# Another order of loads in the opening of a streaming encoder step: input rows first, scale vectors by ScalarE's queue, weight pieces split on ScalarE

## The chip, the cores and the metric

The kernel runs on one core of one Trainium2 chip. Its time is the device time of one execution in microseconds (us); the time before is the median of three runs. The profile is one further execution, with the hardware profiler on. TensorE (PE) multiplies matrices, VectorE (DVE), ScalarE (ACT) and GpSimd (POOL) work element by element, and SyncE (SP) issues most of the transfers (DMA). Matrices come from on-chip SBUF and their products go to PSUM banks.

## The reference

A two-layer streaming encoder, for a prompt of 1024 rows and for 8 running streams of 16 rows each (together one more tile of 128 rows, the "sample" tile). All is float32.

```python
def project_a(x, g_norm, w_qkv, g_q, g_k):            # layer 0
    qkv = rmsnorm(x, g_norm) @ w_qkv                  # 1024 -> 1024 q + 256 k + 256 v
    q, k, v = jnp.split(qkv, ...)
    return rmsnorm(q per head, g_q), rmsnorm(k per head, g_k), v

for layer in range(2):
    # layer 0: window attention with distance penalty and learned sinks, own chunk of 64 rows + 2 before
    # layer 1: own q; K/V computed once from the layer's input; own chunk + 8 before; relative bias
    hp = hp + attention(hp) @ w_o                     # prompt, hs the same with the cached keys
    hp = hp + jnp.square(jax.nn.relu(rmsnorm(hp, g_mlp) @ w_up)) @ w_down
```

`rmsnorm(x, g)` is `x * rsqrt(mean(x*x) + 1e-6) * g`. The outputs are the two streams' rows and the new keys and values.

## The kernel before

The 1024 prompt rows are eight tiles of 128 rows (0 to 7), the sample tile is number 8 (`ST`). To keep float32 accuracy each operand of a product is split in an upper part of reduced mantissa (`hh`, or `w[:, 0]`) and the rest (`hl`, `w[:, 1]`), and a product is three matmuls: upper by upper, upper by rest, rest by upper.

A layer has an attention stage (`attention`), an output projection (`wo_phase`) and an MLP (`mlp_up`, `mlp_down`). The change concerns the opening of layer 0's attention, between the program's start and about 55 us.

The opening goes so. `prep_gains` loads the five scale vectors in five transfers (L1153), has TensorE turn them (`ps_g`) and VectorE copy them to `gcol`, one column for each block of 128 features. `X(t)` loads the rows of tile t (L1331). `N(t)` has TensorE turn them, eight transposes into two PSUM banks `ps_n` (L191), has ScalarE and VectorE split them into `hh` and `hl` (L109, L115), and takes the sum of squares on ScalarE (L182, `junk`). `load_block` loads 1024x512 weights as four transfers of 512 KB into four buffers `raw` and `raw2` and splits each with `split_g`: the scaled upper part on GpSimd (L166), the rest on VectorE (L171). `K1(t)` is the K/V projection of a tile, 8 chunks of three matmuls (L198, L199, L200) into a bank `ps_mm`, followed by the work that empties this bank: V to `VS` on ScalarE and VectorE (L257, L258), K to `kw` twice on ScalarE (L264, L265), and its norm. `Q1(t, 0)` is the projection of the first half of the heads, with weights `wq[0]`, followed by its own norm. K1 of tiles 0, 1 and ST run chunk by chunk together, and then Q1 of the three one after the other. K1(0) and Q1(0) use the one bank of the role `m`, the others the two banks of the role `s`. `K2` and `Q2` turn K and Q. `spill(t)` writes `hh` and `hl` to DRAM (`hTd`, L1361) for the second half of the heads later on. `sinks` loads the constants `cst` and the sinks, and prepares `usink`, `susink` and others for the scores. `unit` is the attention of a pair of sample streams; it loads cached keys and values (`kc`, `vc`).

The order in which each engine gets its instructions is not the text's order: a scheduler sets it by a timeline of its own, from data dependencies, priorities and `behind(a, b)`, which puts instruction b after a in that timeline without a wait on the chip. Each engine then runs its own list strictly in order. SP, too, issues its transfers in order, and an issue waits until its buffer is free and until the transfer eight before it has landed.

Of the kernel before, what the change touches and what calls it, by code (L numbers as in the profile page):

```python
# [75 lines left out]
class Build:  # L76
# [45 lines left out]
    def load_block(self, dst, w, n0, g, ks=range(0, KC, 2), act=False):  # L122
        nc = self.nc
        wr = w.rearrange("(k p) n -> p k n", p=P)
        for k0 in ks:
            raw = self.raw([P, 2, 512])
            nc.sync.dma_start(raw, wr[:, k0 : k0 + 2, n0 : n0 + 512])
            split = lambda k0=k0, raw=raw: self.split_g(
                dst[:, 0, k0 : k0 + 2, :], dst[:, 1, k0 : k0 + 2, :], raw, g, k0, act
# [31 lines left out]
    def split_g(self, hi, lo, raw, g, k0, act):  # L161
        nc = self.nc
        for k in range(raw.shape[1]):
            s = self.gcol[:, g * KC + k0 + k : g * KC + k0 + k + 1]
            if "g" in self.engs and not act:
                nc.gpsimd.tensor_scalar(hi[:, k], raw[:, k], s, 1.0, ALU.mult, ALU.mult)  # L166
            else:
                z = nc.scalar.activation(hi[:, k], raw[:, k], AF.Copy, scale=s)
                if act:
                    self.behind(self.lp, z)  # L170
# [347 lines left out]
    def unit(self, up, small, layer, bp, j, v8, gq8, cache_k, cache_v):  # L518
        nc = self.nc
        kc = up.tile([P, 2, HD], F32, tag="kc", name="kc")  # L520
        nc.sync.dma_start(kc, cache_k[2 * bp : 2 * bp + 2, :, j, :].rearrange("b k d -> k b d"))
        vc = up.tile([P, 2, HD], F32, tag="vc", name="vc")
        nc.sync.dma_start(vc, cache_v[2 * bp : 2 * bp + 2, :, j, :].rearrange("b k d -> k b d"))
# [620 lines left out]
    def prep_gains(self):  # L1144
        nc, I = self.nc, self.ins
        with ExitStack() as st:
            self.psum_pools(st, "pg", dict(m=(1, 1)), dict(m="m"))
            tmp = self.pool(st, "tmpg")
            g = tmp.tile([5 * KC, P], F32, tag="g", name="g")
            for i, v in enumerate(  # L1150
                (I["g_attn"][0], I["g_attn"][1], I["g_mlp"][0], I["g_mlp"][1], I["g_kv"])
            ):
                nc.sync.dma_start(g[i * KC : (i + 1) * KC, :], v.rearrange("(k p) -> k p", p=P))  # L1153
            ps = self.psum("m", [P, 5 * KC], "ps_g")
            nc.tensor.transpose(ps, g, self.ident[0 : 5 * KC, 0 : 5 * KC])
            nc.vector.tensor_copy(self.gcol, ps)
# [11 lines left out]
    def run(self):  # L1168
# [9 lines left out]
        with ExitStack() as top:  # L1178
# [40 lines left out]
            self.prep_gains()  # L1219
# [31 lines left out]
    def sinks(self, ring):  # L1251
        nc, I = self.nc, self.ins
        self.cst = ring.tile([P, C_W], F32, tag="cst", name="cst")
        nc.sync.dma_start(self.cst, I["consts"])
        self.sink = ring.tile([P, H], F32, tag="sink", name="sink")
        nc.sync.dma_start(self.sink, I["sink_a"][0].partition_broadcast(P))
        self.usink = ring.tile([P, H], F32, tag="usink", name="usink")
        nc.vector.tensor_tensor(self.usink, self.sink, self.cst[:, C_ISL : C_ISL + H], ALU.mult)
# [3 lines left out]
        for i in range(G):  # L1262
            nc.sync.dma_start(
                self.ssink[i * 32 : i * 32 + 32, :],
                sk[i : i + 13 : 4].partition_broadcast(32),
            )
        self.nslope = ring.tile([P, KV], F32, tag="nslope", name="nslope")
# [6 lines left out]
    def attention(self, layer):  # L1274
# [18 lines left out]
        with ExitStack() as st:  # L1293
# [307 lines left out]
            if 1 in psp:  # L1601
                wq[0] = self.wslot()
                for k0 in range(0, KC, 2):
                    self.load_split(wq[0], 1, [k0, k0 + 1])
# [202 lines left out]
```

## Time and profile before

| | |
|---|---|
| median of 3 runs | 2391.8 us (2388.46 to 2393.51) |
| the profiled execution | 2387.86 us |
| its span, first to last instruction | 2386.1 us |
| TensorE busy | 2313.9 us, 97% of the span |
| VectorE, ScalarE, GpSimd busy | 1627.6, 1216.5, 540.8 us |
| mean rate of all transfers | 161 GB/s |

A row of a timeline gives start, length, engine, source line, operation and tiles, and in brackets how long the engine stood idle before it and what released it. A row "0.00:50.00" of a table by stretches gives the length of the stretch, the busy time of PE, PE's weight loads, DVE, ACT and POOL with the number of instructions, the granted TensorE clock as a share of full speed, the busy share of the DMA engines and their GB/s. "SPq" and "ACTq" rows are the issue of a transfer, not the transfer. A matmul's row is longer than its distance to the next, since matmuls overlap.

### The profile page before, as it was taken

How to read it: one execution, taken by the hardware profiler on the slowest of the kernel's cores; microseconds unless marked ns; L12 is line 12 of the kernel's file. 1: busy time of each engine (PE TensorE's matmuls, PEld its weight loads, DVE VectorE, ACT ScalarE, POOL GpSimd, SP SyncE). 2: the span in 40 equal slices, each digit the busy share in tenths (PEclk: the TensorE clock that was granted, in tenths of full speed). 3: DMA queues.
4: the chain of work that ended last, by engine and by line, in shares of the span. 5: the costliest groups of instructions: out<-in, count | busy, mean ns of one | idle time of the engine just before them, and what ended most of it. 6: DMA issues, size and time to landing. Idle time of an engine off the chain costs nothing.

```text
span 2386.1 us, 33438 instructions
## 1 busy us (share of the span) xinstructions
PE 2313.9 (97%) x11621; PEld 1931.7 (81%) x11621; DVE 1627.6 (68%) x3002; ACT 1216.5 (51%) x2423; POOL 540.8 (23%) x828
## 2 busy tenths in 40 slices
PE   7998999899999999999999999998999999999999
PEld 6787877788888878888778788887888888888887
DVE  6788786655565776776577876877555565777674
ACT  3777674555555432332267666665555555323321
POOL 4334332311221100000333444444111211000000
PEclk9999999999999999999999999999999999999999
DMA  7335545343443964333653655554443445734332
GB/s 258 119 108 169 170 146 200 129 146 126 157 146 123 356 213 149 119 128 109 232 153 112 198 166 167 168 168 169 142 142 129 158 145 203 274 133 159 117 113 115
DMA packets 217529, 383.78 MB, mean 161 GB/s; under 512 B 50248, under 2 KB 124944, under 8 KB 210192
## 3 DMA queue, kind: packets, MB, share of 16 engines
q1 hardware_dynamic: 194288, 305.08, 38.9%
q0 software_dynamic: 21776, 71.84, 7.8%
q10 hardware_dynamic: 1296, 4.72, 0.5%
q8 instruction: 92, 1.51, 0.3%
q14 instruction: 77, 0.63, 0.1%
HBM read 245.42 MB, written 135.09 MB: 159 GB/s over the span
## 4 chain that ended last, share of the span: by engine, by line
PE 79%; DVE 7%; DMA 7%; ACT 3%; issue 2%; POOL 1%; SPq 1%; ACTq 0%; DVEq 0%; POOLq 0%
PE ps_x L727 9%; PE ps_x L729 9%; PE ps_x L728 9%; PE ps_y L729 7%; PE ps_y L728 7%; PE ps_y L727 7%; PE ps_mm L198 3%; PE ps_mm L200 3%; PE ps_mm L199 3%; PE ps_tr L305 2%; PE ps_mm L157 1%; PE ps_mm L158 1%; PE ps_mm L159 1%; PE ps_s L729 1%; PE ps_s L728 1%
## 5 line engine op out<-in xcount | busy, mean ns | idle before, releaser
L109 ACT CAST w<-r 128x2048 fp32r<-128x2048 f32 x56 | 107.1, 1913 | 325.2 <-PE ps_y L729 213.0
L727 PE MATMUL ps_x<-w,s 128*128 128x512 f32 x512 | 199.6, 390 | 4.2 <-DVE hc L866 2.1
L729 PE MATMUL ps_x<-w,s 128*128 128x512 f32 x512 | 199.4, 389 | 0.0
L728 PE MATMUL ps_x<-w,s 128*128 128x512 f32 x512 | 199.3, 389 | 0.0
L198 PE MATMUL ps_mm<-w,hh 128*128 128x512 f32 x432 | 172.5, 401 | 7.3 <-POOL w L166 3.2
L200 PE MATMUL ps_mm<-w,hl 128*128 128x512 f32 x432 | 172.1, 399 | 1.6 <-DVE hl L115 0.8
L199 PE MATMUL ps_mm<-w,hh 128*128 128x512 f32 x432 | 170.9, 397 | 1.3 <-DVE w L171 1.1
L109 ACT CAST s<-s 128x2048 fp32r<-128x2048 f32 x56 | 107.1, 1913 | 118.1 <-DMA s<-hd 109.3
L115 DVE TENSOR_TENSOR w<-r,w 128x2048 fp32r<-128x2048 f32 x56 | 128.2, 2290 | 51.0 <-ACT w L109 51.0
L727 PE MATMUL ps_x<-sx,w 128*128 128x512 f32 (+1 forms) x408 | 157.9, 387 | 3.9 <-ACT hc L846 3.0
L1033 DVE TENSOR_TENSOR x<-ps_y,x 128x512 f32<-128x512 f32 x136 | 92.4, 687 | 100.8 <-PE ps_y L729 100.8
L729 PE MATMUL ps_x<-sx,w 128*128 128x512 f32 (+1 forms) x408 | 154.2, 378 | 0.0
L728 PE MATMUL ps_x<-sx,w 128*128 128x512 f32 (+1 forms) x408 | 154.1, 378 | 0.0
L109 ACT CAST w<-ru 128x512 fp32r<-128x512 f32 (+1 forms) x160 | 110.0, 708 | 85.5 <-PE ps_y L728 32.0
L729 PE MATMUL ps_y<-w,s 128*128 128x512 f32 x384 | 149.5, 389 | 0.0
L727 PE MATMUL ps_y<-w,s 128*128 128x512 f32 x384 | 149.4, 389 | 0.0
L728 PE MATMUL ps_y<-w,s 128*128 128x512 f32 x384 | 149.4, 389 | 0.0
L115 DVE TENSOR_TENSOR s<-s 128x2048 fp32r<-128x2048 f32 x56 | 128.0, 2286 | 29.1 <-ACT s L109 28.9
L115 DVE TENSOR_TENSOR ptl<-ps_tr,pth 128x512 fp32r<-128x512 f32 x180 | 122.5, 685 | 24.1 <-ACT pth L109 17.8
L115 DVE TENSOR_TENSOR w<-ru,w 128x512 fp32r<-128x512 f32 (+1 forms) x160 | 126.5, 793 | 11.2 <-ACT w L109 11.1
L115 DVE TENSOR_TENSOR wq<-ru,wq 128x1024 fp32r<-128x1024 f32 x32 | 39.7, 1240 | 131.9 <-ACT wq L109 131.9
L109 ACT CAST pth<-ps_tr 128x512 fp32r<-128x512 f32 x180 | 104.9, 595 | 45.0 <-PE ps_tr L305 36.7
(280 smaller groups left out, 6579.7 us busy)
## 6 DMA issues: line engine op xcount, KB each, us to landing
s<-hd SPq DMA_DIRECT2D x56, 1024.0 KB, 4.7
ru<-in_w_up SPq DMA_DIRECT2D x64, 512.0 KB, 4.0
r<-in_w_down SPq DMA_DIRECT2D x32, 1024.0 KB, 5.8
hd<-hc POOLq DMA_DIRECT2D x128, 256.0 KB, 2.7
hd<-hs POOLq DMA_DIRECT2D x96, 256.0 KB, 2.5
x<-xd SPq DMA_DIRECT2D x41, 512.0 KB, 4.4
o<-oTd SPq DMA_DIRECT2D x52, 256.0 KB, 5.0
xd<-xo SPq DMA_DIRECT2D x18, 512.0 KB, 2.8
```

The costliest lines, as they stand in the source:

```text
L109: a = nc.scalar.copy(hi, src)
L115: return a, e.tensor_tensor(lo, src, hi.bitcast(F32), ALU.subtract)
L157: nc.tensor.matmul(ps, oh[:, k, :], w[:, 0, k, nn], start=(k == 0), stop=False)
L158: nc.tensor.matmul(ps, oh[:, k, :], w[:, 1, k, nn], start=False, stop=False)
L198: nc.tensor.matmul(ps, a, w[:, 0, k, :], start=(k == 0), stop=False)
L199: nc.tensor.matmul(ps, a, w[:, 1, k, :], start=False, stop=False)
L200: self.lp = nc.tensor.matmul(ps, b, w[:, 0, k, :], start=False, stop=(k == KC - 1))
L305: self.lp = nc.tensor.transpose(pt[:, i, :], get(i), self.ident)
L727: a = mm(ps, ah, bh, start=first, stop=False, skip_group_check=True)
L728: mm(ps, ah, bl, start=False, stop=False, skip_group_check=True)
L729: return a, mm(ps, al, bh, start=False, stop=last, skip_group_check=True)
L1033: tt(xs[t][:, N[n]], ps, xs[t][:, N[n]], ALU.add)
```

## The change

It moves the scale vectors out of a stage of their own: three transfers (two vectors each, and one) are issued by ScalarE's queue, after which SP's first transfers are the identity and tile 0. They are turned only after tile 0's rows. The weights for K/V come as pieces of 256 KB (`parts=2`), in turn with the rows of tiles 0, 1 and ST, and ST has a buffer of its own. In layer 0 the upper parts of all weights are now scaled on ScalarE instead of GpSimd (`eng='cu'`). Constants, rows of tiles 2 and 3, sinks, spills of tiles 0, 1, ST and the caches are put behind the last weight transfer (`self.gate`), in layer 1 the caches and the MLP's scale vector as well. Sinks are prepared after Q1(1).

```diff
     def load_block(self, dst, w, n0, g, ks=range(0, KC, 2), parts=1):
...
-            nc.sync.dma_start(raw, wr[:, k0 : k0 + 2, n0 : n0 + 512])
+            for k in range(0, 2, 2 // parts):
+                z = slice(k, k + 2 // parts)
+                self.gate = nc.sync.dma_start(raw[:, z], wr[:, k0 : k0 + 2, n0 : n0 + 512][:, z])
...
-            if "g" in self.engs and not act:
+            if "g" in self.engs:
                 nc.gpsimd.tensor_scalar(hi[:, k], raw[:, k], s, 1.0, ALU.mult, ALU.mult)
             else:
                 z = nc.scalar.activation(hi[:, k], raw[:, k], AF.Copy, scale=s)
-                if act:
+                if self.pace:
                     self.behind(self.lp, z)
...
+    def load_gains(self, pool):
+        g = pool.tile([5 * KC, P], F32, tag="pvt", name="g", bufs=1)
+        n = 2 * KC
+        for i, v in enumerate((I["g_attn"], I["g_mlp"])):
+            nc.scalar.dma_start(g[i * n : (i + 1) * n, :], v.rearrange("l (k p) -> (l k) p", p=P))
+        nc.scalar.dma_start(g[2 * n :, :], I["g_kv"].rearrange("(k p) -> k p", p=P))
...
             if A:
+                g = self.load_gains(apool)
                 X(0)
-                self.load_block(wkv, wkv_src, kv0, gkv, [0])
+                N(0)
+                self.turn_gains(g)
+                self.load_block(wkv, wkv_src, kv0, gkv, [0], 2)
                 X(1)
-                N(0)
-                self.load_block(wkv, wkv_src, kv0, gkv, [2])
+                self.load_block(wkv, wkv_src, kv0, gkv, [2], 2)
                 X(ST)
                 N(1, "pt")
-                self.load_block(wkv, wkv_src, kv0, gkv, [4, 6])
+                self.load_block(wkv, wkv_src, kv0, gkv, [4, 6], 2)
                 N(ST, "p")
...
-            if A:
-                self.sinks(ring)
...
                 weave(K1(0), K1(1, "s"), K1(ST, "s"))
+                self.cst = ring.tile([P, C_W], F32, tag="cst", name="cst")
+                self.behind(self.gate, nc.sync.dma_start(self.cst, I["consts"]))
...
+            if A:
+                X(2)
+                X(3)
             spill(0)
             run(Q1(0, 0))
             K2(0)
             spill(1)
             run(Q1(1, 0, "s"))
+            if A:
+                self.sinks(ring)
...
-    dict(banks=dict(g=(5, 1), s=(2, 1), m=(1, 1)), ... eng='cgu', ...
+    dict(banks=dict(g=(5, 1), s=(2, 1), m=(1, 1)), ... eng='cu', ...
```

The first place is SP's list at the program's start. Before it was this:

```order
L1188 DMA eye<-in_eye 128x128
L1153 DMA g<-in_g_attn 8x128 x2
L1153 DMA g<-in_g_mlp 8x128 x2
L1153 DMA g<-in_g_kv 8x128
L1331 DMA x<-in_x_prompt 128x1024 x2
L127 DMA raw_267<-in_w_qkv_a 128x2x512
L127 DMA raw<-in_w_qkv_a 128x2x512 x2
L127 DMA raw_305<-in_w_qkv_a 128x2x512
L606 DMA gk<-in_g_k_a 128x64
L606 DMA gq<-in_g_q_a 128x64
L1254 DMA cst<-in_consts 128x596
L1256 DMA sink<-in_sink_a 128x16
```

Now the same place, where `x` is a tile's rows and the shape shows the pieces:

```order
L1193 DMA eye<-in_eye 128x128
L1339 DMA x<-in_x_prompt 128x1024
L129 DMA raw<-in_w_qkv_a 128x512 x2
L1339 DMA x<-in_x_prompt 128x1024
L129 DMA raw_258<-in_w_qkv_a 128x512 x2
L1339 DMA x<-in_x_sample 128x1024
L129 DMA raw<-in_w_qkv_a 128x512 x2
L129 DMA raw_298<-in_w_qkv_a 128x512 x2
L610 DMA gk<-in_g_k_a 128x64
L610 DMA gq<-in_g_q_a 128x64
L129 DMA raw<-in_w_qkv_a 128x2x512
L129 DMA raw_341<-in_w_qkv_a 128x2x512
```

The scale vectors are gone from it, tile 0 stands second, and constants and sinks no longer stand ahead of the Q weights (the last two rows).

The second place is TensorE's list at the end of the K/V projection of tile 0, whose bank is `ps_mm_383` before and `ps_mm_359` now. Before, its last three matmuls are followed by those of tile 1 (`ps_mm_387`) and 24 of the sample tile (`ps_mm_391`), and only then comes Q of tile 0:

```order
L198 MATMUL ps_mm_383<-w_234,hh_245 128x512
L199 MATMUL ps_mm_383<-w_234,hh_245 128x512
L200 MATMUL ps_mm_383<-w_234,hl_246 128x512
L198 MATMUL ps_mm_387<-w_234,hh_276 128x512
L198 MATMUL ps_mm_391<-w_234,hh_311 128x512
L199 MATMUL ps_mm_391<-w_234,hh_311 128x512
L199 MATMUL ps_mm_387<-w_234,hh_276 128x512
L200 MATMUL ps_mm_387<-w_234,hl_278 128x512
```

Now the three tiles end together, and Q of tile 0 (`ps_mm_488`, the same bank) follows:

```order
L200 MATMUL ps_mm_359<-w_217,hh_224 128x512
L201 MATMUL ps_mm_359<-w_217,hh_224 128x512
L202 MATMUL ps_mm_359<-w_217,hl_225 128x512
L200 MATMUL ps_mm_363<-w_217,hh_268 128x512
L201 MATMUL ps_mm_363<-w_217,hh_268 128x512
L202 MATMUL ps_mm_363<-w_217,hl_270 128x512
L200 MATMUL ps_mm_367<-w_217,hh_305 128x512
L201 MATMUL ps_mm_367<-w_217,hh_305 128x512
L202 MATMUL ps_mm_367<-w_217,hl_306 128x512
L200 MATMUL ps_mm_488<-w_334,hh_224 128x512
L201 MATMUL ps_mm_488<-w_334,hh_224 128x512
L202 MATMUL ps_mm_488<-w_334,hl_225 128x512
```

Between tile 0's last K/V matmul and its first Q matmul stood 27 others, and now six.

The third place is ScalarE's list about 200 us into the program, the first rows after the opening that differ there. `qn` and `qr` empty a bank of the Q projection, `pth` is the upper part of turned probabilities, `pts` and `so` belong to a sample unit. Before:

```order
L338 COPY pvt<-ps_pv 64x512
L109 CAST qT<-ps_q 64x4x128
L590 COPY pts<-ps_utp 128x384
L109 CAST pth<-ps_tr 128x512
L109 CAST qT<-ps_q 64x2x4x32
L207 ACTIVATE qn<-ps_mm 128x512
L208 COPY qr<-ps_mm 128x512
L109 CAST qT<-ps_q 64x2x4x32
L599 COPY so<-ps_uo 64x64 x2
L109 CAST pth<-ps_tr 128x512
```

And now:

```order
L340 COPY pvt<-ps_pv 64x512
L109 CAST qT<-ps_q 64x4x128
L209 ACTIVATE qn<-ps_mm 128x512
L594 COPY pts<-ps_utp 128x384
L109 CAST pth<-ps_tr 128x512
L109 CAST qT<-ps_q 64x2x4x32
L210 COPY qr<-ps_mm 128x512
L603 COPY so<-ps_uo 64x64 x2
L109 CAST qT<-ps_q 64x2x4x32
L109 CAST pth<-ps_tr 128x512
```

`qn` has moved ahead of the sample's and the probabilities' copies. From here to the end of layer 0's attention every engine's list differs in such ways, and in a few rows of layer 1.

81 lines of the change are left out of this document (44 added, 37 removed).

## The prediction

> **What bounds the kernel now.** The page's first lines come first, then the table of engine-busy time in 50-us stretches.
>
> ```profile
> span 2386.1 us, 33438 instructions
> PE 2313.9 (97%) x11621; PEld 1931.7 (81%) x11621; DVE 1627.6 (68%) x3002; ACT 1216.5 (51%) x2423; POOL 540.8 (23%) x828
> ...
> 0.00:50.00 50.00, 39.48 (x170) 32.29 (x171) 30.62 (x62) 14.13 (x29) 23.66 (x33) 1.00 0.71 255
> ...
> 150.00:200.00 50.00, 46.48 (x255) 37.08 (x253) 43.74 (x130) 38.42 (x107) 19.28 (x30) 1.00 0.51 150
> 200.00:250.00 50.00, 46.04 (x253) 38.72 (x253) 40.94 (x134) 35.70 (x109) 20.65 (x37) 0.97 0.46 148
> ...
> 400.00:450.00 50.00, 43.27 (x257) 35.90 (x256) 43.44 (x63) 28.34 (x52) 21.65 (x18) 1.00 0.36 128
> ...
> 500.00:550.00 50.00, 50.00 (x251) 42.43 (x251) 29.16 (x42) 28.37 (x47) 8.70 (x16) 1.00 0.37 127
> ...
> 1150.00:1200.00 50.00, 44.32 (x210) 36.69 (x209) 28.85 (x65) 17.98 (x39) 17.75 (x20) 0.97 0.70 240
> ```
>
> TensorE (first column behind the length) is the bound: a stretch of the MLP shows 50.00 of 50. What TensorE loses, it loses in the attention stages and above all at the start, 10.52 us in the first 50. No clock time stands in the program, so a shorter start should move all that follows forward, and a full TensorE behind it carries that to the end.
>
> The opening itself is read from TensorE's timeline.
>
> ```profile
> 6.51 3.65 PE L191 MATMUL ps_n<-identr,x 128*128 128x128 f32 x16 [2.17 <-DMA x<-in_x_prompt]
> ...
> 13.38 1.22 PE L198 MATMUL ps_mm<-w,hh 128*128 128x512 f32 x2 [3.22 <-POOL w L166]
> 15.68 0.80 PE L199 MATMUL ps_mm<-w,hh 128*128 128x512 f32 x1 [1.08 <-DVE w L171]
> ...
> 17.13 0.63 PE L200 MATMUL ps_mm<-w,hl 128*128 128x512 f32 x1
> 17.56 1.05 PE L198 MATMUL ps_mm<-w,hh 128*128 128x512 f32 x2
> ...
> 20.17 0.39 PE L198 MATMUL ps_mm<-w,hh 128*128 128x512 f32 x1
> 20.40 0.39 PE L199 MATMUL ps_mm<-w,hh 128*128 128x512 f32 x1
> ...
> 22.67 1.04 PE L191 MATMUL ps_n<-identr,x 128*128 128x128 f32 x8
> ...
> 33.99 0.39 PE L198 MATMUL ps_mm<-w,hh 128*128 128x512 f32 x1
> ```
>
> Sixteen transposes (rows 0 and 1) end at 10.16; then TensorE waits 3.22 us for the upper and 1.08 us for the lower part of the first weight chunk, 4.30 us together, and works without a gap until 33.99, the first matmul of the Q projection of row tile 0. At the start a matmul follows the one before by 0.43 us (17.13 to 17.56), later by 0.23 (20.17 to 20.40): the array runs at half speed at first.
>
> **Part by part.** What sets the first wait is the queue of loads.
>
> ```profile
> 0.74 0.39 SPq L1188 DMA_DIRECT2D eye<-in_eye  x1
> 1.19 0.68 SPq L1153 DMA_DIRECT2D g<-in_g_attn  x2
> ...
> 2.92 0.83 SPq L1331 DMA_DIRECT2D x<-in_x_prompt  x2
> ...
> 6.40 1.06 ACT L182 ACTIVATE junk<-x 128x1024 bf16<-128x1024 f32 x1 [4.38 <-DMA x<-in_x_prompt]
> ...
> 8.00:12.00 4.00, 2.16 (x11) 1.76 (x9) 2.64 (x5) 2.78 (x6) 2.06 (x4) 1.00 1.03 377
> 12.00:16.00 4.00, 1.54 (x3) 0.82 (x4) 4.00 (x6) 0.00 (x0) 4.00 (x5) 1.00 0.57 205
> 20.00:40.00 20.00, 20.00 (x95) 16.64 (x94) 12.33 (x25) 4.18 (x10) 9.62 (x14) 1.00 1.04 389
> ```
>
> *Rows first, scale vectors on the other queue.* Five small issues stand between the identity and tile 0. Without them tile 0 is issued at 1.19 instead of 2.92, so it lands 1.73 us earlier: 6.40 becomes 4.67. Two weight pieces (0.52 MB) now stand ahead of tile 1 (0.52 MB). At 377 GB/s (8 to 12 us) each takes 1.4 us, so tile 1 lands at 7.5; with the 1.9 us that tile 1 needed at most before (its transposes start by 8.34, half way through the sixteen), at 8.0. I take 7.7. Eight transposes at 3.65/16 = 0.23 us end at 9.5: **0.6 us earlier** than 10.16. ScalarE's three issues end before it needs tile 0:
>
> ```profile
> L667 ACTq DMA_DIRECT2D xd<-x x5: 326/326/344, 404.2 to 431.8; - x5
> L168 ACT ACTIVATE w<-raw,gcol x8: 707/714/744, 166.2 to 180.1; 128x512 fp32r<-128x512 f32 x8
> L171 DVE SCALAR_TENSOR_TENSOR w<-raw,gcol,w x16: 735/1171/1179, 11.1 to 35.5; 128x512 fp32r<-128x512 f32 x16
> ```
>
> *Small pieces, split on ScalarE.* ScalarE's own issue costs 0.33 us, three of them 1.0, against 4.67. Then: squares of tile 0 to 5.9, two casts to 7.2, the scales about 7.5, two splits at 0.71 us to 8.9. VectorE's lower parts take 0.74 each when GpSimd does not work beside it (the 1.17 are those beside GpSimd's splits) and end at 9.7. So the first chunk is ready when the transposes end, and **the waits of 4.30 us go**. Later chunks: six splits, three casts and two squares of 1.06 end at 17.5, while TensorE, at 0.23 us a matmul, asks for the last one at about 26. The eight splits for Q (5.7 us on ScalarE, 4.18 of 20 us busy in 20 to 40) end near 24; the first is wanted at 30. The covers are 8 and 6 us; beyond them each late microsecond costs one. GpSimd's sixteen splits vanish off the path.
>
> *x_sample early.* Its transposes now stand behind only seven projection matmuls, reached at 9.5 + 7 x 0.43 = 12.5. It lands after tile 1 and one more weight pair, 2.8 us behind 7.7, at 10.5: two microseconds of cover, no cost.
>
> *A new wait.* The last matmuls of K/V of the three tiles now stand together, and Q of tile 0 right behind them; it needs the bank that K/V of tile 0 used. The rows that free that bank:
>
> ```profile
> 28.13 0.47 ACT L257 ACTIVATE VS<-ps_mm,rx 128x256 fp32r<-128x256 f32 x1 [3.75 <-POOL w L166]
> ...
> 31.62 0.47 DVE L258 SCALAR_TENSOR_TENSOR VS<-ps_mm,rx,VS 128x256 fp32r<-128x256 f32 x1
> ...
> 32.13 0.37 ACT L264 COPY kw<-ps_mm 128x256 f32<-128x256 f32 x1 [2.39 <-DVE VS L258]
> 32.40 0.39 ACT L265 ACTIVATE kw<-ps_mm 128x256 f32<-128x256 f32 x1
> ```
>
> Before, 27 matmuls lay over this; now six. From the issue of the last matmul of tile 0: 0.39 to its end, tile 1's VS to 1.6 (it waits for its own product), the two kw to 2.3; TensorE would go on at 7 x 0.23 = 1.6. **Plus 0.7 us**; below 0 it cannot be, above 1.5 only if ScalarE is late. Queued behind it are Q of tiles 0, 1 and x_sample, which wait as one.
>
> *The slow stretch after the first Q projections.*
>
> ```profile
> 54.32 0.66 PE L241 MATMUL ps_q<-identr,qr 128*128 128x128 f32 x4 [1.80 <-DVE qr L220]
> ...
> 56.00:59.00 3.00, 3.00 (x9) 2.27 (x9) 2.91 (x5) 1.87 (x4) 0.40 (x1) 0.54 1.00 378
> ```
>
> After a wait of 1.80 us the granted clock falls to 0.54 for 3 us: 1.4 us lost. Whether it comes back 5 us earlier in the run I can't tell; I take half, **minus 0.7**, bounds 0 and 1.4.
>
> *Loads behind the gate* (sinks, constants, caches, spills) leave the ring in the first 15 us and come at 20 to 40. The 20 to 40 stretch already moves 389 GB/s with TensorE at 20.00 of 20, so a busy ring there hides under TensorE. *In layer 1* cache and g_mlp loads move behind its weights; nothing waits for them there, and of the 5.68 us that TensorE lacks in 1150 to 1200 I let them change none, at most 1 either way. *The order in the attention* differs on every engine from about 200 us on; the three quoted attention stretches lack 3.52 + 3.96 + 6.73 = 14.2 us. I count 0, and a third of that, 4.7, as the bound on either side.
>
> Sum: -0.6 - 4.3 + 0.7 - 0.7 = **-4.9 us**. The profiled execution took 2387.86 us, 1.8 over its span, so 2383.0; it lies 3.9 below the median of the three runs, 2391.8, which becomes **2386.9**.
>
> The 389 GB/s of 20 to 40 were moved with transfers of 256 and 512 KB in flight together, so I keep 377 for the pieces. A rule speaks against them: the Trainium skill, "DMA: Bandwidth & Descriptors", section Bandwidth, wants transfers of 1 MiB or more for three quarters of the peak and gives 32% at 64 KB. By it, pieces at half of its 435 GB/s (an estimate from that page) bring tile 1 about 2 us later, and the sum would be -2.9.
>
> **Rivals.**
>
> *The pieces move more slowly* (0.05). At the 205 GB/s of 12 to 16 us, 1.05 MB take 5.1 instead of 2.8 us, and tile 1 comes 2.3 later: -2.6, 2389.2. For it: that stretch is the one with many small transfers. Against it: in it the queue was waiting, not the ring. It is what the skill's rule above would do here.
>
> *The clock rises later* (0.17). The array speeds up after about 3 us of matmuls (15.68 to 18.6). Now eight transposes of x_sample fall into that time. If they don't help the clock up, they cost 8 x 0.23 less the 1.04 of the row at 22.67, 0.8 us, and four more slow matmuls 0.8: -3.3, 2388.5. The Trainium skill, "TensorE: Matmul & The Clock Gate", section Part 4, says that transposes don't count as activity; the sixteen here ended with the array still slow, which fits but has a second reading, too short a run.
>
> *The sinks come late* (0.10). Their loads now follow the spills, and VectorE's susink stands amid the K work of tile 0 and x_sample, GpSimd's first cache product behind loads that wait for the sinks.
>
> ```profile
> 11.55 3.88 SPq L1263 DMA_DIRECT2D ssink<-in_sink_a  x4
> ...
> 21.08 0.16 DVE L1272 TENSOR_TENSOR susink<-ssink,rsl 128x4 f32<-128x4 f32 x1 [0.29 <-DMA ssink<-in_sink_a]
> ```
>
> Issue to use took 9.5 us. Issued near 28 (behind the Q weights at 22 and two tiles' spills, 2.1 MB at 389 GB/s), they are there at 37.5, and VectorE comes to susink at about 38.5. The Q transposes that need what follows are due 4 us after that; 9 us more than before would cost 4: -0.9, 2390.9.
>
> *The new order costs more than the opening gains* (0.14). From 200 us on ScalarE gets the probabilities' casts behind other work. A wait of that kind stands there once:
>
> ```profile
> 206.50 0.80 PE L312 MATMUL ps_pv<-pth,VS 128*128 128x512 f32 x1 [2.49 <-ACT pth L109]
> ```
>
> Four more of them, 10.0 us, eat the gain and pass the upper bound of "same"; five, one in each of five of the steps that follow, give -4.9 + 12.5 = +7.6, 2399.4. Against it: the reordered rows are the same instructions, and some waits there should shrink.
>
> *More is gained* (0.08). The clock rises as early as 12 us (up to 2 us of the slow 13.38 to 18.6), the slow stretch goes wholly (0.7 more) and the order helps by 1.4: -9.0, 2382.8. That the change would not do what it says can be left out: the new order shows each of its moves.
>
> **How the numbers follow.** The forecast has 0.46. The range runs from -4.9 - 2.7 (clock, slow stretch) - 3.7 of order, -11.3, 2380.5, to the sinks' case and 4.0 of order, +3.1, 2394.9; it leaves out most of the reorder rival and little below. The three runs lie 5.05 us, 0.2%, apart, about what a measurement of this kernel can tell from no change; 0.2% is 4.8 us. The forecast lies just beyond: of its 0.46 I count 0.36 faster and 0.10 same; the pieces 0.05 same; the clock 0.03 and 0.14; the sinks 0.09 same, 0.01 slower; the order 0.14 slower; more 0.08 faster. Faster 0.47, same 0.38, slower 0.15.
>
> **What would show it.** Right: transposes of tile 0 from about 4.7, no wait over 0.5 us between tile 1's transposes and a wait of 0.7 for ScalarE's kw ahead of Q of tile 0, which starts at 33.99 - 0.6 - 4.3 + 0.7 = 29.8. Wrong: TensorE waiting for ScalarE's w or for x_sample before 15 us; susink or the cache product waiting for DMA; or TensorE's sum over 150 to 450 changed by more than 5 us.

## The result: slower by 0.2%, with a shorter opening and a longer attention

The changed kernel takes 2393.82 us (median of 22 runs, 2388.16 to 2399.34), the kernel before beside it 2388.59 us (22 runs, 2383.78 to 2395.57): a ratio of 1.0021, 95% interval 1.0014 to 1.0028. Its profiled execution took 2392.92 us. The median of the three runs of before that the prediction started from, 2391.8, lay 3.2 us above the median of the 22. The medians and ranges of the cut kernels further down leave out runs more than 1.5% above the fastest of the same cut (two of six of `o_before`, one of five of `o_after`, four of six of `o_gpsimd`, one of six of `o_no_gate`); with them they are 134.87, 132.72, 132.87 and 132.86 us, and the expectations name the first two, rounded.

The first lines of the changed kernel's page:

```profile
span 2391.1 us, 33419 instructions
...
PE 2319.0 (97%) x11621; PEld 1936.2 (81%) x11621; DVE 1623.4 (68%) x3002; ACT 1222.9 (51%) x2439; POOL 525.8 (22%) x812
```

TensorE's timeline in the changed kernel's opening (start, length, line, operation, and in brackets the wait ahead of it and what ended it):

```profile
5.37 1.94 PE L193 MATMUL ps_n<-identr,x 128*128 128x128 f32 x8 [5.37 <-DMA x<-in_x_prompt]
8.40 1.97 PE L193 MATMUL ps_n<-identr,x 128*128 128x128 f32 x8 [0.84 <-DMA x<-in_x_prompt]
10.03 0.78 PE L200 MATMUL ps_mm<-w,hh 128*128 128x512 f32 x1
...
11.03 0.50 PE L202 MATMUL ps_mm<-w,hl 128*128 128x512 f32 x1
11.36 0.40 PE L200 MATMUL ps_mm<-w,hh 128*128 128x512 f32 x1
...
27.68 0.39 PE L202 MATMUL ps_mm<-w,hl 128*128 128x512 f32 x1
28.56 0.50 PE L200 MATMUL ps_mm<-w,hh 128*128 128x512 f32 x1 [0.49 <-ACT kw L267]
48.18 0.44 PE L243 MATMUL ps_q<-identr,ks 128*128 128x128 f32 x2 [2.45 <-DVE ks L285]
52.83 1.11 PE L243 MATMUL ps_q<-identr,qr 128*128 128x128 f32 x4 [1.95 <-DVE qr L222]
```

The first weights are there when the transposes end (10.03, no wait), and Q of tile 0 starts at 28.56 where it started at 33.99: 5.43 us earlier, 1.2 more than forecast. (This execution is the earliest of its kind: in the fifteen profiles below that have these loads and the splits on ScalarE, Q of tile 0 starts at 28.56 to 30.13.) Then two waits follow that no term of the sum held. K of the changed kernel is turned at 48.18 behind 2.45 us of waiting, and Q at 52.83 instead of 54.32. Of the 5.43 us there are 1.49 left. GpSimd's timeline shows who is late; its row of before comes first:

```profile
36.41 0.45 POOL L539 TENSOR_TENSOR kc<-kc,gq 128x128 f32<-128x128 f32 x1
```

and these are the rows of the changed kernel, GpSimd's and then SP's:

```profile
42.68 0.46 POOL L543 TENSOR_TENSOR kc<-kc,gq 128x128 f32<-128x128 f32 x1 [8.88 <-DMA kc<-in_cache_k_a]
...
44.00 1.64 POOL L221 TENSOR_TENSOR qrs<-qms,mhalf 128x8 f32<-128x8 f32 x1
45.60 1.01 POOL L273 TENSOR_TENSOR krs<-kms,mhalf 128x4 f32<-128x4 f32 x1
```

```profile
30.01 2.99 SPq L1266 DMA_DIRECT2D ssink<-in_sink_a  x4
...
35.95 0.38 SPq L523 DMA_DIRECT2D kc<-in_cache_k_a  x1
```

SP comes to the cached keys `kc` at 35.95, behind spills and sinks. GpSimd, which runs its list in order, stands 8.88 us at the product with them, and behind it wait the factors `qrs` and `krs` of the opening's own Q and K, whose inputs VectorE had begun at 36.35 and 38.48 (`qms`, `kms`). The clock falls in the waits; stretches of 4 us (length; busy time of PE, its weight loads, DVE, ACT, POOL; granted clock; DMA share; GB/s), of before:

```profile
52.00:56.00 4.00, 2.04 (x14) 1.59 (x13) 3.67 (x11) 3.98 (x10) 2.31 (x3) 1.00 0.78 259
56.00:60.00 4.00, 4.00 (x12) 3.08 (x12) 3.26 (x6) 2.46 (x5) 0.40 (x1) 0.57 0.86 323
```

and of the changed kernel, the loads' two stretches at the start as well:

```profile
4.00:8.00 4.00, 2.19 (x9) 1.74 (x9) 1.15 (x5) 2.38 (x5) 0.56 (x1) 1.00 1.01 391
8.00:12.00 4.00, 3.60 (x14) 3.27 (x15) 3.42 (x7) 4.00 (x8) 0.55 (x1) 1.00 1.04 400
...
48.00:52.00 4.00, 2.70 (x14) 2.30 (x14) 3.38 (x10) 2.78 (x7) 2.39 (x2) 0.60 0.33 88
52.00:56.00 4.00, 3.17 (x11) 2.79 (x12) 3.83 (x9) 3.95 (x9) 1.96 (x3) 0.50 0.91 318
56.00:60.00 4.00, 4.00 (x13) 3.15 (x12) 2.29 (x4) 0.98 (x2) 0.00 (x0) 0.62 0.81 289
```

One slow stretch has become three. Yet this only eats the gain. The loss comes after 150 us, as two rows of VectorE show that bracket the rest of layer 0's attention, the eighth `qr` (the Q projection of a tile, first half of the heads, times its factors) and the first addition of the output projection's stage (`x`), first of before, then of the changed kernel:

```profile
157.04 0.68 DVE L220 TENSOR_TENSOR qr<-qr,qrs 128x512 f32<-128x512 f32 x1
...
389.45 0.69 DVE L665 TENSOR_TENSOR x<-ps_wo,x 128x512 f32<-128x512 f32 x1 [0.81 <-PE ps_wo L159]
```

```profile
158.08 0.68 DVE L222 TENSOR_TENSOR qr<-qr,qrs 128x512 f32<-128x512 f32 x1
...
396.66 0.69 DVE L669 TENSOR_TENSOR x<-ps_wo,x 128x512 f32<-128x512 f32 x1 [1.43 <-PE ps_wo L161]
```

From the one to the other it is 232.41 us before and 238.58 now: 6.2 us longer, with the same instructions in another order (1194 matmul records of TensorE in the one as in the other).

### The profile page after: what moved, and what is told of

It reads as the page before. It is cut to its first block, busy times and chain, and to the rows that moved or that the text cites. A ratio compares the mean times of both kernels' runs of the same rounds, so it can differ in the third digit from the quotient of the medians.

```text
span 2391.1 us, 33419 instructions
## 1 busy us (share of the span) xinstructions
PE 2319.0 (97%) x11621; PEld 1936.2 (81%) x11621; DVE 1623.4 (68%) x3002; ACT 1222.9 (51%) x2439; POOL 525.8 (22%) x812
## 4 chain that ended last, share of the span: by engine, by line
PE 83%; DVE 6%; DMA 5%; ACT 3%; issue 1%; POOL 1%; SPq 0%; ACTq 0%; DVEq 0%; POOLq 0%
PE ps_x L731 9%; PE ps_x L733 9%; PE ps_x L732 9%; PE ps_y L731 7%; PE ps_y L733 7%; PE ps_y L732 7%; PE ps_mm L200 3%; PE ps_mm L202 3%; PE ps_mm L201 3%; PE ps_tr L307 2%; PE ps_mm L159 1%; PE ps_mm L161 1%; PE ps_mm L160 1%; PE ps_pv L314 1%; PE ps_s L733 1%
```

## Experiments

Two theories. *Keys*: the late `kc` holds GpSimd, and that eats the opening's gain. *Order*: the new order of the attention behind it loses time by itself. All experiments but `o_gpsimd` and `o_no_gate` hold each engine's list fixed as the scheduler had made it (order only, no wait on the chip), so that a single row can be moved and all else stays.

### One cause at a time in the whole kernel

`e1_pool` takes GpSimd's wait away from the factors of Q and K, by moving the products behind them on GpSimd:

```diff
 TENSOR_TENSOR krs<-kms,mhalf 128x4 x2
-TENSOR_TENSOR kc<-kc,gq 128x128
-CAST uks<-kc 128x2x64
-TENSOR_TENSOR uks<-kc,uks 128x2x64
 TENSOR_TENSOR qrs<-qms,mhalf 128x8
 TENSOR_TENSOR krs<-kms,mhalf 128x4
-TENSOR_TENSOR kc<-kc,gq 128x128
 TENSOR_TENSOR qrs<-qms,mhalf 128x8 x2
 TENSOR_TENSOR rx<-vx,mhalf 128x1 x2
+TENSOR_TENSOR kc<-kc,gq 128x128
+CAST uks<-kc 128x2x64
+TENSOR_TENSOR uks<-kc,uks 128x2x64
+TENSOR_TENSOR kc<-kc,gq 128x128
```

> The changed kernel with every engine's list fixed to what it was, but for four rows on GpSimd: the three products that prepare the first cached keys (kc, uks twice) and the one of the second kc stand behind the norms qrs and krs of the three opening tiles instead of ahead of them. Theory (GpSimd's strict order): in the changed kernel GpSimd stood 8.88 us for the cached keys, and qrs and krs, queued behind, came 6 to 7 us late; TensorE then waited 2.45 us at 48.18. Without that the wait for ks goes, the slow clock from 48 to 59 shrinks to the one stretch of 3 us that the kernel before has, and the matmuls at 62 us come about 4.9 us earlier: 2393.8 - 4.9 = about 2389 us, ratio to the kernel before 1.000; 1.6 us less again if the slow stretch at 76 us goes too. Rival (the Q and K work is late because the transfers are late or the ring is full, GpSimd's order being only a symptom): TensorE's waits at 48 and 53 us stay and the time stays near 2394. Rival (the loss is in the order of the attention alone): no change beyond 1 us.

`e2_cache_early` leaves GpSimd alone and moves the load of the first unit's caches forward on SP:

```diff
 DMA x<-in_x_prompt 128x1024 x2
+DMA kc<-in_cache_k_a 128x2x64
+DMA vc<-in_cache_v_a 128x2x64
 DMA hTd_120<-hh 128x512
...
 DMA raw_2411<-in_w_qkv_a 128x2x512
 DMA gb<-in_g_mlp 128x1024
-DMA kc<-in_cache_k_a 128x2x64
-DMA vc<-in_cache_v_a 128x2x64
 DMA kc<-in_cache_k_a 128x2x64
```

> The changed kernel with every engine's list fixed to what it was, but for two rows on SP: the loads of the first cached keys and values (kc, vc) stand right behind the rows of tiles 2 and 3, at about 21 us, ahead of the spills and the sinks, instead of at 36 us. GpSimd's list is unchanged. Theory: the keys then land before GpSimd asks at 33.8 us, its wait of 8.88 us goes, and the gain is the same as with the rows moved on GpSimd, 4 to 5 us, about 2389; up to 1 us less, since GpSimd still does 1.2 us of key work ahead of qrs. Rival (a full ring delays whatever is loaded there): kc still lands after 38 us and less than 2 us is won.

`e3_order` keeps the changed opening and gives all engines, from about 110 us to layer 0's MLP, their lists of before. ScalarE's begins so:

```diff
 CAST qT<-ps_q 64x4x128
-ACTIVATE qn<-ps_mm 128x512
 COPY pts<-ps_utp 128x384
 CAST pth<-ps_tr 128x512
 CAST qT<-ps_q 64x2x4x32
+ACTIVATE qn<-ps_mm 128x512
 COPY qr<-ps_mm 128x512
-COPY so<-ps_uo 64x64 x2
 CAST qT<-ps_q 64x2x4x32
+COPY so<-ps_uo 64x64 x2
```

> The changed kernel, whose engines' lists are as they were up to about 110 us and from layer 0's MLP on; between the two (the rest of layer 0's attention and its output projection) they are those of the kernel before. Theory: this order lost 4.65 us in the profile (work that came 1.45 us late at 190 us came 6.1 us late at 480 us), so the time is 2393.8 - 4.65 = about 2389 us. Rival (the work between is late because it starts in another phase against the transfers and the clock, whatever its order): no change beyond 1 us.

`e4_both` makes the edits of `e1_pool` and `e3_order` together.

> Both edits: the four key products behind qrs and krs on GpSimd, and the order of the kernel before in layer 0's attention. Theory: the two losses add up, 2393.8 - 4.9 - 4.65 = about 2384 us, 4 to 5 us below the kernel before (ratio 0.998), which is what was forecast for the change. Rival (one loss hides the other, since a step that is late anyway covers what is late in front of it): no better than the better one of the two alone, 2389.

Measured, beside 2389.05 us of before: `e1_pool` 2397.15 us (ratio 1.0040, 1.0026 to 1.0055), `e2_cache_early` 2395.24 (1.0027, 1.0017 to 1.0037), `e3_order` 2392.63 (1.0015, 1.0003 to 1.0026), `e4_both` 2398.34 (1.0037, 1.0025 to 1.0049). Not one gained what its theory said. The first two failed for reasons that their traces show. `e1_pool`, GpSimd, SP and TensorE:

```profile
51.88 0.46 POOL L543 TENSOR_TENSOR kc<-kc,gq 128x128 f32<-128x128 f32 x1
```

```profile
53.26 0.37 SPq L523 DMA_DIRECT2D kc<-in_cache_k_a  x1
53.72 0.71 SPq L296 DMA_DIRECT2D KT<-KT  x1
```

```profile
57.35 0.44 PE L363 MATMUL ps_s<-KT,qT 128*128 128x128 f32 x1 [6.34 <-DMA KT<-KT]
```

The product came at 51.88, and only behind it and its split was the one buffer of `kc` free for the second unit's load; SP stood at that load until 53.26, the copies of turned K (`KT`) stood behind it on SP, and TensorE waited 6.34 us for them. The wait had changed its queue. `e4_both` has the same edit and the same wait, 6.28 us. `e2_cache_early`, GpSimd and TensorE:

```profile
49.11 0.46 POOL L543 TENSOR_TENSOR kc<-kc,gq 128x128 f32<-128x128 f32 x1 [7.69 <-DMA kc<-in_cache_k_a]
49.53 3.24 POOL L221 TENSOR_TENSOR qrs<-qms,mhalf 128x8 f32<-128x8 f32 x2
```

```profile
51.94 0.66 PE L243 MATMUL ps_q<-identr,qr 128*128 128x128 f32 x4 [4.16 <-DVE qr L222]
```

The first product no longer waits, but the second does, 7.69 us, and it stands ahead of two further `qrs`. So the two edits have to go together: `e6_keys_both` loads the first caches early, and on GpSimd moves the second product alone behind the last `rx`:

```diff
-TENSOR_TENSOR kc<-kc,gq 128x128
 TENSOR_TENSOR qrs<-qms,mhalf 128x8 x2
 TENSOR_TENSOR rx<-vx,mhalf 128x1 x2
+TENSOR_TENSOR kc<-kc,gq 128x128
```

> The same two edits in the whole changed kernel. Theory: what the cut kernel wins comes on to the end, 2393.8 - 4.5 = about 2389.3 us. Rival (the steps behind the opening wait for transfers that keep their own pace, so that a gain ahead of them is given back): 2392 to 2395.

Measured: 2389.39 us beside 2386.81, ratio 1.0011 (1.0000 to 1.0021). Against the changed kernel's 1.0021 (1.0014 to 1.0028) that would be 2.4 us better, but the intervals overlap; it is still not faster than before.

### The opening by itself

Whole-kernel runs scatter by some 10 us. Kernels that end behind the first three steps of layer 0's attention scatter by about 2 to 3:

```diff
+                if s == 3:
+                    return None
```

> The kernel before, cut off behind the first three steps of layer 0's attention (the first 549 rows of TensorE's list, each engine's list as in the whole kernel; all that follows, and so most of the outputs, is left out). It takes some 120 us. It stands beside the same cut of the changed kernel: their difference is what the opening alone is worth, without the 5 us by which whole executions differ among themselves.

> The changed kernel, cut off at the same place (the rest is left out). Theory (the opening wins 5.4 us up to Q of tile 0 and loses it again to the cached keys on GpSimd and a longer stretch of slow clock): as long as the kernel before's cut within 2 us, and so the 5 us by which the whole kernel is slower are lost behind it. Rival (the opening itself is the loss): 3 to 5 us longer. Rival (the opening keeps its gain): 4 to 5 us shorter.

> The changed kernel cut off at the same place, with kc and vc of the first sample unit loaded right behind the rows of tiles 2 and 3, and GpSimd's product for the second kc behind the norms qrs and krs of the opening. With the one edit alone the wait moved: with the rows moved on GpSimd to the copies of KT, which stand on SP behind the second kc, whose load waits for the first product (one buffer); with the early load alone to GpSimd's second product. Theory: with both edits no wait of that family is left but the 1.80 us that the kernel before has at 54 us, and the opening keeps its gain: 4 to 5 us shorter than the changed kernel's cut. Rival (the ring is the bound of the opening, and some transfer is late in any order): less than 2 us shorter.

Measured: before 134.14 us (133.68 to 135.41), changed 132.45 (131.75 to 133.14), with both edits for the keys 130.30 (129.32 to 131.19). These ranges do not touch. The changed opening gains 1.7 us, and 3.8 without the late keys; 2.1 us is their price in this cut, and the 2.4 us of the whole kernel agree with it without being clear of its scatter. The stretch around the waits, of the three in this order (the profiled execution of `o_before`, 136.86 us, is its longest):

```profile
44.00:64.00 20.00, 18.05 (x85) 14.70 (x84) 11.52 (x25) 8.90 (x19) 6.22 (x7) 0.91 0.43 126
```

```profile
44.00:64.00 20.00, 16.35 (x80) 13.52 (x79) 14.46 (x42) 10.45 (x28) 7.25 (x8) 0.91 0.44 130
```

```profile
44.00:64.00 20.00, 17.20 (x88) 14.05 (x87) 11.26 (x35) 10.07 (x27) 7.02 (x10) 1.00 0.35 107
```

Two parts of the change were undone alone in this cut, with the scheduler free. `o_gpsimd` scales the weights' upper parts on GpSimd again:

```diff
-    dict( ... eng='cu', ...
+    dict( ... eng='cgu', ...
```

> The changed kernel cut off behind the first three steps of the attention (the rest is left out), with one part undone: the upper parts of the weights are scaled on GpSimd again, as in the kernel before; rows first, scale vectors by ScalarE's queue, small pieces and the gate stay. If the splits on ScalarE bring the gain (the 4.3 us of the forecast): 2 to 4 us longer than the changed kernel's cut (132.7), at or above that of the kernel before (134.9), Q of tile 0 starting at 31 to 33 us instead of 28.6. If the order of the loads brings it: within 1 us of 132.7.

Measured: 129.90 and 131.44 us. TensorE's rows at the first weights and at Q of tile 0, and the latter row of `o_after`:

```profile
9.99 0.78 PE L200 MATMUL ps_mm<-w,hh 128*128 128x512 f32 x1
...
30.29 0.47 PE L200 MATMUL ps_mm<-w,hh 128*128 128x512 f32 x1 [0.52 <-ACT kw L267]
```

```profile
30.05 0.50 PE L200 MATMUL ps_mm<-w,hh 128*128 128x512 f32 x1 [0.47 <-ACT kw L267]
```

The wait of 4.3 us stays away with GpSimd splitting, and the cut is no longer than `o_after`, where the theory asked for 2 to 4 us more: the loads' order removed it, not the splits on ScalarE. `o_no_gate` takes the gate away:

```diff
-        self.behind(self.gate, d)
+        pass
```

> The same cut with another part undone: constants, rows of tiles 2 and 3, spills, sinks and caches are not put behind the last weight transfer, so that spills and sinks go between the Q weights again, as in the kernel before; the sinks are still prepared after Q of tile 1 and the cached keys still loaded after them. If the gate is what makes the keys late: GpSimd's wait for kc shrinks and it is 1 to 3 us shorter than 132.7. If it is the later place of the sinks and keys in the program: within 1 us. If the Q weights need the gate (a late piece stops TensorE): 1 to 3 us longer.

Measured: 132.78 us (131.15 to 133.09). TensorE and GpSimd, and GpSimd's row of `o_after`:

```profile
35.41 0.50 PE L200 MATMUL ps_mm<-w,hh 128*128 128x512 f32 x1 [1.78 <-ACT w L170]
```

```profile
37.49 0.46 POOL L543 TENSOR_TENSOR kc<-kc,gq 128x128 f32<-128x128 f32 x1 [6.55 <-DMA kc<-in_cache_k_a]
```

```profile
41.51 0.46 POOL L543 TENSOR_TENSOR kc<-kc,gq 128x128 f32<-128x128 f32 x1 [6.22 <-DMA kc<-in_cache_k_a]
```

Without the gate the keys come 4 us earlier, GpSimd, which has come to them earlier as well, still waits 6.55 us, and TensorE now waits 1.78 us for Q weights. So the gate does what it is for and makes the keys later; the cut's time does not tell the two apart. GpSimd's wait itself also comes from the load's place behind spills and sinks, which `e2_cache_early` and `e6_keys_both` moved.

### The attention's order by itself

These cuts end behind layer 0's output projection. `l_before` and `l_after` are the two kernels; `l_order` has the changed opening with before's lists from 110 us on, `l_order_on_before` the opening of before with the changed lists; `l_keys_both` and `l_keys_order` have the opening of `e6_keys_both` with the changed lists and with before's.

> The kernel before, cut off behind the output projection of layer 0 (both MLPs and layer 1 are left out, and with them most outputs; every engine's list up to there as in the whole kernel). Some 450 us. It stands beside the same cut of the changed kernel.

> The changed kernel, cut off at the same place. The opening alone was 2.2 us shorter than before's (132.7 against 134.9), the whole kernel is 5 us longer, so 7 us are lost between. Theory (the new order of layer 0's attention loses them): 4 to 6 us longer than the kernel before's cut. Rival (they are lost in layer 1, where cached keys and values and the MLP's scale vector are now loaded behind the weights): 1 to 3 us shorter, as the opening. Third (half and half): 1 to 2 us longer.

> The cut behind layer 0's output projection (both MLPs and layer 1 left out): the changed kernel's opening, and from about 110 us on the order of the kernel before. If the new order alone is the loss: the opening's gain is left, 445.9 - 2.2 = about 443.8 us. If any order that starts at another time loses as much: 448 to 450, as the changed kernel's cut (449.2).

> The same cut with the opening of the kernel before and, from about 110 us on, the order of the changed kernel. If the new order is the loss: 445.9 + 5.4 = about 451 us. If not: 445 to 447, as the kernel before's cut (445.9).

> The same cut, the changed kernel with both edits on the cached keys (opening 4.6 us shorter than before's), in the changed kernel's order. If openings and orders add up: 449.2 - 2.4 = about 446.8 us. If the steps behind give the gain back: 449.

> The same cut, the changed kernel with both edits on the cached keys and, from about 110 us on, the order of the kernel before. If openings and orders add up: 445.9 - 4.6 = about 441.4 us, the shortest of all. If a gain in front is given back: 444 to 446.

Measured, medians of four or five runs with their ranges (`l_before` and `l_after` in one session, the other four in the next, where the whole kernel before took 2387.65 and 2389.86 us):

| opening | attention in before's order | in the changed order | the order's price |
|---|---|---|---|
| before | 445.94 (445.17 to 447.30) | 452.16 (448.31 to 454.69) | +6.2 |
| changed | 447.39 (444.57 to 449.53) | 449.16 (448.04 to 450.18) | +1.8 |
| keys early | 443.33 (441.65 to 444.89) | 449.93 (445.59 to 450.85) | +6.6 |

With two of the three openings the changed order costs over 6 us; with the third, that of the changed kernel itself, it is 1.8 us and the ranges overlap. The profiles show a price with all three. From the `qr` row to the addition in `x`, the profiles with before's order (`before`, `e3_order`, `e4_both`, `l_before`, `l_order`, `l_keys_order`, and `e7_rest_of_before` below) take 231.77 to 235.32 us, mean 233.5; those with the changed order (`after`, `e1_pool`, `e2_cache_early`, `e6_keys_both`, `l_after`, `l_order_on_before`, `l_keys_both`, and `e8_layer1_of_before` below) 235.99 to 240.47, mean 238.1. That is 4.6 us, without an overlap; with the changed opening alone (`after`, `l_after`, `e8_layer1_of_before` against `e3_order`, `l_order`) it is 4.3. Where it lies is read among the chunks of the output projection that run beside the attention, from the stretch 340 to 400 us; before's order (`l_before`, then `l_keys_order`):

```profile
340.00:400.00 60.00, 56.06 (x283) 44.53 (x284) 41.80 (x109) 33.13 (x88) 18.16 (x30) 1.00 0.53 180
```

```profile
340.00:400.00 60.00, 56.23 (x289) 45.38 (x288) 40.06 (x93) 31.24 (x77) 16.32 (x26) 1.00 0.59 201
```

the changed order (`l_after`, then `l_order_on_before`):

```profile
340.00:400.00 60.00, 53.40 (x274) 42.43 (x273) 38.79 (x104) 31.13 (x83) 16.58 (x29) 1.00 0.50 166
```

```profile
340.00:400.00 60.00, 52.67 (x271) 41.97 (x271) 38.83 (x105) 30.59 (x82) 16.05 (x28) 1.00 0.51 167
```

TensorE lacks about 3 us more there at a full clock; over all fifteen profiles its mean in the stretch is 56.1 us with before's order and 53.4 with the changed one. Its waits over a microsecond in `l_after`, and rows of VectorE:

```profile
352.47 0.50 PE L159 MATMUL ps_mm<-w,oh 128*128 128x512 f32 x1 [1.72 <-DVE xo L1557]
...
367.23 0.47 PE L159 MATMUL ps_mm<-w,oh 128*128 128x512 f32 x1 [1.64 <-DVE xo L1557]
...
373.11 0.50 PE L159 MATMUL ps_mm<-w,oh 128*128 128x512 f32 x1 [1.36 <-DVE xo L1557]
```

```profile
351.72 0.69 DVE L1557 TENSOR_TENSOR xo<-ps_mm,xo 128x512 f32<-128x512 f32 x1 [2.12 <-DMA xo<-in_x_prompt]
...
371.76 0.69 DVE L115 TENSOR_TENSOR ol<-o,oh 128x512 fp32r<-128x512 f32 x1 [1.23 <-ACT oh L109]
372.37 0.68 DVE L1557 TENSOR_TENSOR xo<-ps_mm,xo 128x512 f32<-128x512 f32 x1
```

and in `l_before`, where one wait over a microsecond stands in this stretch:

```profile
366.93 0.47 PE L157 MATMUL ps_mm<-w,oh 128*128 128x512 f32 x1 [1.55 <-DVE xo L1544]
```

```profile
352.06 0.69 DVE L1544 TENSOR_TENSOR xo<-ps_mm,xo 128x512 f32<-128x512 f32 x1 [0.51 <-DMA xo<-in_x_prompt]
```

The chunks of the output projection share one bank; VectorE empties it by adding it to the tile's rows `xo`, and those are loaded again from DRAM. TensorE stands still until the addition. Once the addition is late for that load (351.72), once it stands in VectorE's list behind a split that waits for ScalarE (371.76, then 372.37). TensorE's waits for `xo` of over 0.6 us between 300 and 400 us sum to 1.6, 1.6, 1.6 and 3.4 us in `before`, `l_before`, `l_order` and `l_keys_order`, and to 4.6, 5.4, 3.9 and 5.6 us in `after`, `l_after`, `l_order_on_before` and `l_keys_both`: 2.8 us more on average. That this chain makes up all of the 4.6 us is not shown; it holds about 3 of them.

### The rest of the program

`e8_layer1_of_before` keeps the changed lists up to the middle of layer 0's MLP and follows before's from there, without the gate in layer 1. `e7_rest_of_before` has the opening of `e6_keys_both` and before's lists from about 110 us to the end. Both hold back by the gate in layer 0 alone:

```diff
-        self.behind(self.gate, d)
+        if layer == 0:
+            self.behind(self.gate, d)
```

> The changed kernel up to the middle of layer 0's MLP; from there on every engine's list is the kernel before's (in layer 1 the cached keys, cached values and the MLP's scale vector are no longer held behind the weights). Theory (loss in layer 0's attention): as the changed kernel, ratio to the kernel before 1.002, within 1 us. Rival (loss in layer 1): 4 to 7 us below the changed kernel, ratio 0.999 to 1.0005.

> The opening of the changed kernel with both edits on the cached keys (its cut took 130.3 us against 134.9 of the kernel before), and from about 110 us to the end every engine's list as in the kernel before. If the lists behind the opening cost the time, whichever of them: 4.6 us below the kernel before, ratio 0.998. Rival (the same lists, started 4.6 us earlier, meet their transfers and the clock in another phase and give the gain back): ratio 0.9995 to 1.001.

Measured: `e8_layer1_of_before` 2393.14 us, ratio 1.0015 (1.0005 to 1.0025), not to be told from the changed kernel's 1.0021; its interval is too wide for the one or two microseconds in question. `e7_rest_of_before` 2385.60 us beside 2387.65, ratio 0.9990 (0.9981 to 0.9999): the one version that is faster than both kernels. Its bracket of the attention:

```profile
151.32 0.68 DVE L222 TENSOR_TENSOR qr<-qr,qrs 128x512 f32<-128x512 f32 x1
...
386.64 0.69 DVE L671 TENSOR_TENSOR x<-ps_wo,x 128x512 f32<-128x512 f32 x1 [0.85 <-PE ps_wo L161]
```

It comes to `qr` 5.7 us ahead of before, and to the addition 2.8 us ahead: before's order gives back about half of a lead that it was not made for (235.32 us against 232.41). Beside `e6_keys_both`, which has the same opening, it is the clearest measure of the order in the whole kernel: 2.6 us above before there (2389.39 less 2386.81), 2.05 below it here, 4.6 us between them, and the two intervals do not overlap. Layer 1's lists differ between the two as well; `e8_layer1_of_before` shows no gain from them that is clear of its scatter.

## Why the prediction was wrong

The time came at 2393.82 us, 6.9 above the forecast's 2386.9 and on the other side of no change. That it lies within the range is luck: the range hung on a time before of 2391.8, and from 2388.59 its upper end would have been 2391.7. The sum was -4.9 us, and +5.2 came (2393.82 less 2388.59). By the medians of the cuts it came so: -1.7 at the end of the opening, +3.2 behind layer 0's output projection (449.16 less 445.94), +5.2 at the end. Two steps failed, the loads behind the gate and the order in the attention, both counted at 0.

- **The two waits of 4.30 us** are gone, as forecast, but not for the reason given. The step credited the splits on ScalarE; `o_gpsimd` shows that the order of the loads does it alone.
- **Tile 1 earlier, -0.6.** Tile 0 came at 5.37 (forecast 4.7) and tile 1 at 8.40 (forecast 7.7). The first product starts at 10.03, where the sum had the transposes end at 9.5; in the kernel before they ended at 10.16. The term is -0.1.
- **The new wait, +0.7.** From 27.68 to 28.56 are 0.88 us where 0.23 would be: +0.65, right in size and cause.
- **The clock at the start.** From 11.03 to 11.36 are 0.33 us, and soon 0.23: the array is fast from about 11.4 us, not from 18.6. The rival "more is gained" had it at 12 us, for up to 2 us; with the 0.5 lost at tile 1 that leaves the 1.2 us beyond the forecast. How much of it came is chance of the execution: in `o_after` matmuls are still 0.43 us apart at 12.6, and Q of tile 0 starts at 30.05, against 29.8 forecast. The rival in which the clock rises later fell.
- **The pieces** came, between the rows of the tiles, at 391 and 400 GB/s, where 377 was taken. The Trainium skill, "DMA: Bandwidth & Descriptors", section Bandwidth, asks for transfers of 1 MiB or more; the loss that this implies for smaller ones did not show here for 256 KB with several in flight.
- **Loads behind the gate, 0.** The first step that failed. "A busy ring there hides under TensorE" asked how fast the ring is, and not who stands in line behind the load. The rival named the place ("GpSimd's first cache product behind loads that wait for the sinks") and a cost of 4 us; the cuts show 2.1 us (-1.7 with the late keys, -3.8 without). Its mechanism was right, its chance of 0.10 too small.
- **The slow stretch, -0.7.** Wrong sign: half of a loss was written off at a wait that the same change made longer (three slow stretches instead of one). Part of that hung on the keys: with them early the clock stays at 1.00 from 44 to 64 us in `o_keys_both`, `e6_keys_both`, `e7_rest_of_before` and `l_keys_order`, but it fell in `l_keys_both`.
- **The order in the attention, 0.** The second step that failed, and by most measures the larger one. It was counted at nothing, with a bound of 4.7 us on either side (drawn also from 400 to 450 us, which lies behind the attention), because "the reordered rows are the same instructions, and some waits there should shrink". The cuts show +4.9 between the end of the opening and the end of the output projection (3.2 and 1.7). With before's order behind the same opening (`l_order`) 3.2 of these 4.9 stay. With the lists swapped, the price is 6.2, 1.8 and 6.6 us by the opening, 4.6 in the brackets, and 4.6 in the whole kernel with the keys early (`e6_keys_both` against `e7_rest_of_before`). The rival's waits were looked for at ScalarE's casts near 206 us; some 3 us of them stand at the output projection's bank, near 340 to 375. Its size, +12.5, was too large.
- **Layer 1, ±1.** Open. Some 2 us of the whole difference (5.2 less 3.2) arise behind layer 0's projection; no run had an interval small enough to place them.
- **The test by TensorE's sum over 150 to 450** said nothing: 281.46 us before, 280.87 now. A stretch with fixed borders shows idle time and not progress, because work slides over its borders.

With both failed steps undone (`e7_rest_of_before`) the ratio falls from 1.0021 to 0.9990, 7.4 us and clear of both intervals; 2 us of the forecast 4.9 are won. How the 7.4 us divide is open, for one thing speaks against a simple sum of keys and order: before's order behind the changed opening as it is brings back only 1.2 us in the whole kernel (`e3_order`, intervals overlapping) and 1.8 in the cut (`l_order`). The profiled execution of `e3_order`, at 2401.38 us the slowest of its twelve, is level with before at the addition in `x` (389.23 against 389.45) and loses its time behind it. TensorE and the stretch there:

```profile
433.42 1.09 PE L678 MATMUL ps_n<-identr,s 128*128 128x128 f32 x4 [3.19 <-DVE sx L115]
```

```profile
432.00:436.00 4.00, 2.58 (x12) 2.61 (x13) 3.77 (x6) 1.45 (x3) 1.29 (x1) 0.50 0.32 130
```

In the profile of before this wait is 1.89 us (at 431.30) and the clock is at 1.00 in the stretch. Whether such a loss follows from the place of the transfers or from chance of one execution, the runs do not settle.

## What to carry to other kernels

Before a load is moved back, follow its first user's engine: list what stands behind that user in the same in-order list, what waits for its buffer on the issuing queue, and move load and user together, since either alone only shifted the wait here (ratios 1.0040 and 1.0027, against 1.0011 with both). A new order of the same instructions need not be free: where a scheduler redoes 200 us of attention, look for a price at the single-buffered places in it, and try the old order behind the edited opening as well (0.9990, 0.9981 to 0.9999). An opening is best measured in a cut of its own, where 2 us stood clear of the scatter. And read an effect of the clock from several executions: one profile alone showed the opening 1.2 us better than forecast.

## What the hardware showed that was not expected

- When the clock rises differs from execution to execution of one list. The matmuls came to their short distance 1.3 us after the first product in `after` (10.03 to 11.36) and 1.9 us in `e3_order` (10.15 to 12.00), and not within 3 us in `o_after` (9.87, still 0.43 us apart up to the transposes at 13.00). The Trainium skill, "TensorE: Matmul & The Clock Gate", section Part 4, says that transposes do not count as activity as matmuls do. These profiles do not settle it: in all three the first product follows eight transposes without a wait.
- The clock can fall after a wait of 1.80 us that has transposes around it. Between the last product ahead of the wait for `qr` and the first behind it, which start 4.1 us apart (50.60 and 54.73 in `before`), TensorE ran only transposes. With these rows, the wait 1.80 or 1.81 us, the clock fell in `before` (0.57 in 56 to 60 us), `l_before` (0.59) and `o_before` (0.61) and stayed at 1.00 in `l_order_on_before`; it stayed full in `o_keys_both`, `o_gpsimd`, `o_no_gate`, `e6_keys_both`, `e7_rest_of_before` and `l_keys_order` too: the same wait, two outcomes.
- One load of cached keys, 64 KB, took 6.7 us from its issue to its use (35.95 to 42.68), and 8.3 us in `e2_cache_early` (40.76 to 49.11), while spills and weights of 256 to 512 KB were under way as well.
